# Adaptive max pooling on one core: four halving maxima in place of one reduce instruction

## The chip, the cores and the metric

The kernel runs on one core of a Trainium2 chip. The metric is the time of one execution on the device, in microseconds (us); lower is better. Traces come from the hardware profiler, which records one execution.

## The reference

The input is 32 x 256 x 4096 numbers in float32 (134 MB). Each row of 4096 is cut into 256 groups, and the output holds the maximum of each group (8.4 MB).

```python
def reference(x, output_size):            # x: 32 x 256 x 4096, output_size: 256
    batch, channels, length = x.shape
    result = np.zeros((batch, channels, output_size), dtype=np.float32)
    for i in range(output_size):
        start = int(i * length / output_size)
        end = int((i + 1) * length / output_size)
        result[:, :, i] = np.max(x[:, :, start:end], axis=-1)
    return result
```

4096 divides by 256, so every group has exactly W = 16 neighbouring words. In memory the input is a list of 2,097,152 groups of 16 words, and the output one word for each.

## The kernel before

The groups are dealt to the 128 partitions, 16384 groups to each. They come in 17 loads: a first small one of 128 groups per partition (`FIRST`), then loads of 1024 groups (`CHUNK`; one of them has 1020) and a last one of 900 (`last`). The loads belong to two blocks of the output, `group_a` with the first 14 loads and `group_b` with the last 3. A load of 1024 groups is 64 KB per partition, 8.39 MB in all.

Two tiles lie in SBUF. `ring` takes the loads. It has two halves, each of 1024 + 152 groups (`GAP` = 152), and loads go to the halves in turn. Within a half a load starts at offset 0 or at offset 152, in turn (`moved`). So a load shares all but 152 groups of its place with the load two before it. `kept` takes the maxima of all loads but the last; the maxima of the last load (`last_kept`) are written to the end of its own place in `ring`.

Each full load is pooled in two pieces: first the 872 groups (868 for the load of 1020) that the load two places on will overwrite, then the 152 that it won't. The loop writes this order out (`parts`, or `parts[::-1]` where the load is not moved). The load two places on may be issued when the larger piece is done. The first load and the last are pooled in one piece each. This makes 32 calls of `pooled` (line 56), each one VectorE instruction.

All loads are issued from SyncE's queue (SP; line 96, the first at line 87) and wait there for their place in `ring` to come free. Behind them in the same queue are two stores of `kept` (line 117), one for each block; the second of them waits until the last full load is pooled. The maxima of the last load are stored from ScalarE's queue (ACT; line 114). Line 148 is the end of the program, which waits for all stores. No other engine computes; the tile framework places the waits between dependent instructions.

Of the kernel before, what the change touches and what calls it, by code (L numbers as in the profile page):

```python
# [1 line left out]

# [4 lines left out]


@with_exitstack
def kernel(  # L10
    ctx: ExitStack,
    tc: tile.TileContext,
    x: bass.AP,
    output_size: bass.AP,
    out: bass.AP,
):

    nc = tc.nc
    P = nc.NUM_PARTITIONS
    fp32 = mybir.dt.float32

    B, C, L = x.shape
    O = int(output_size)  # L30
    assert L % O == 0, (L, O)
    W = L // O
    total = B * C * O // P
    assert B * C * O % P == 0

    CHUNK = 1024
    GAP = 152
    FIRST = 128
    LOADS_A, LOADS_B = 13, 2

    LESS = 4
    group_a = [FIRST] + [CHUNK] * (LOADS_A - 1) + [CHUNK - LESS]
    last = total - sum(group_a) - LOADS_B * CHUNK
    group_b = [CHUNK] * LOADS_B + [last]
    assert 0 < last and last * (W + 1) <= CHUNK * W

    pool = ctx.enter_context(tc.tile_pool(name="pool", bufs=1))
    ring = pool.tile([P, 2 * (CHUNK + GAP) * W], fp32, tag="ring", name="ring")
    kept = pool.tile([P, total - last], fp32, tag="kept", name="kept")

    xw = x.flatten_outer_dims().rearrange("r (o w) -> (r o) w", w=W)
    ow = out.flatten_outer_dims().rearrange("r o -> (r o)")

    def pooled(dst, at, n):

        nc.vector.reduce_max(  # L56
            out=dst,
            in_=ring[:, at * W : (at + n) * W].rearrange("p (n w) -> p n w", w=W),
            axis=mybir.AxisListType.X,
        )  # L60

    taken = 0

    def group(n):

        nonlocal taken
        span = slice(taken * P, (taken + n) * P)
        taken += n
        return (
            xw[span].rearrange("(p n) w -> p (n w)", p=P),  # L70
            ow[span].rearrange("(p n) -> p n", p=P),
        )

    stores = []
    n_loads = 0
    base = 0
    for g, loads in enumerate((group_a, group_b)):
        xg, og = group(sum(loads))
        a = sum(loads) if g == 0 else 0
        for n in loads:  # L80
            if g == 0:
                a -= n
            xn = xg[:, a * W : (a + n) * W]
            dst = kept[:, base + a : base + a + n] if n != last else None
            if n == FIRST:

                nc.sync.dma_start(  # L87
                    out=ring[:, CHUNK * W : (CHUNK + n) * W], in_=xn
                )
                pooled(dst, CHUNK, n)  # L90
            else:

                low = n_loads % 2 * (CHUNK + GAP)
                moved = n_loads // 2 % 2
                at = low + moved * GAP
                nc.sync.dma_start(out=ring[:, at * W : (at + n) * W], in_=xn)
                if n != last:
                    cut = CHUNK - GAP if moved else GAP
                    parts = [(0, cut), (cut, n)]
                    for u, v in parts if moved else parts[::-1]:  # L100
                        pooled(dst[:, u:v], at + u, v - u)
                else:
                    end = (at + CHUNK) * W
                    last_kept = ring[:, end - n : end]
                    pooled(last_kept, at, n)
                n_loads += 1
            if g:
                a += n
        full = a - last if g else sum(loads)
        stores.append((og[:, 0:full], kept[:, base : base + full]))  # L110
        base += full
    assert taken == total

    nc.scalar.dma_start(out=og[:, full : full + last], in_=last_kept)
    tc.no_sync_barrier()
    for dst, src in stores:
        nc.sync.dma_start(out=dst, in_=src)


# [1 line left out]
_INS = ['x', 'output_size']  # L121
_OUTS = [((32, 256, 256), 'float32')]

_NUMBERS = {'output_size': 256}


# [26 lines left out]
```

## Time and profile before

| what | value |
|---|---|
| median of 3 runs | 334.94 us (334.91 to 335.06) |
| span of the profiled execution | 333.1 us |
| own time of the profiled execution | not listed apart from the runs; median less span is 1.84 us |
| VectorE (DVE) busy | 276.5 us, 83% of the span, 32 instructions |
| DMA | 142.61 MB, mean 428 GB/s over the span |
| loads' queue (q1) | 98.8% of the 16 DMA engines' span |
| HBM read, written | 134.22 MB, 8.39 MB |

How to read the lines in this document: a row of the instruction groups gives the line of the kernel, the engine, the operation, the tile written and the tile read with their shapes, the number of such instructions, then their busy time in us, the mean of one in ns, and the idle time of the engine just before them with what ended it. A row of DMA issues gives the size and the median time from issue to landing. A row of the timeline gives start, duration, and the instruction or the merged run of instructions. A row of the stretches gives the stretch and its length, the busy time of VectorE and of GpSimd with their instructions, the clock granted to TensorE, the mean busy share of the 16 DMA engines and their GB/s.

### The profile page before, as it was taken

How to read it: one execution, taken by the hardware profiler on the slowest of the kernel's cores; microseconds unless marked ns; L12 is line 12 of the kernel's file. 1: busy time of each engine (PE TensorE's matmuls, PEld its weight loads, DVE VectorE, ACT ScalarE, POOL GpSimd, SP SyncE). 2: the span in 40 equal slices, each digit the busy share in tenths (PEclk: the TensorE clock that was granted, in tenths of full speed). 3: DMA queues.
4: the chain of work that ended last, by engine and by line, in shares of the span. 5: the costliest groups of instructions: out<-in, count | busy, mean ns of one | idle time of the engine just before them, and what ended most of it. 6: DMA issues, size and time to landing. Idle time of an engine off the chain costs nothing.

```text
span 333.1 us, 113 instructions
## 1 busy us (share of the span) xinstructions
DVE 276.5 (83%) x32; POOL 0.2 (0%) x4
## 2 busy tenths in 40 slices
DVE  2009979797997979799797979979797998979993
POOL 0000000000000000000000000000000000000000
DMA  9898989899898989899898989899898989899996
GB/s 378 378 504 378 504 378 496 386 441 441 378 504 378 504 378 496 386 457 425 378 504 378 504 378 504 378 441 441 385 494 377 504 378 504 378 458 443 421 413 285
DMA packets 2880, 142.61 MB, mean 428 GB/s; under 512 B 320, under 2 KB 320, under 8 KB 448
## 3 DMA queue, kind: packets, MB, share of 16 engines
q1 hardware_dynamic: 2736, 142.15, 98.8%
q10 hardware_dynamic: 144, 0.46, 0.3%
HBM read 134.22 MB, written 8.39 MB: 428 GB/s over the span
## 4 chain that ended last, share of the span: by engine, by line
DMA 57%; DVE 36%; DVEq 5%; issue 0%; SPq 0%
DMA ring<-in_x_dram 57%; DVE kept L56 36%; DVEq L148 5%; SPq L87 0%
## 5 line engine op out<-in xcount | busy, mean ns | idle before, releaser
L56 DVE TENSOR_REDUCE kept<-ring 128x152 f32<-128x2432 f32 (+3 forms) x31 | 261.4, 8472 | 51.5 <-DMA ring<-in_x_dram 51.5
L56 DVE TENSOR_REDUCE ring<-ring 128x900 f32<-128x14400 f32 x1 | 15.1, 15144 | 0.0
L134 POOL MEMSET const-bfloat16-1.0<- 128x1 bf16 x1 | 0.1, 102 | 0.0
L134 POOL MEMSET const-uint8-127<- 128x1 uint8 x1 | 0.1, 102 | 0.0
L134 POOL MEMSET const-float32-0.0<- 128x1 f32 x1 | 0.1, 99 | 0.2 <-issue 0.2
L134 POOL MEMSET const-float32-1.0<- 128x1 f32 x1 | 0.1, 99 | 0.0
## 6 DMA issues: line engine op xcount, KB each, us to landing
ring<-in_x_dram SPq DMA_DIRECT2D x1, 8160.0 KB, 23.9
ring<-in_x_dram SPq DMA_DIRECT2D x1, 7200.0 KB, 21.6
out_dram<-kept SPq DMA_DIRECT2D x1, 6718.0 KB, 37.2
ring<-in_x_dram SPq DMA_DIRECT2D x1, 1024.0 KB, 4.7
out_dram<-kept SPq DMA_DIRECT2D x1, 1024.0 KB, 18.1
out_dram<-ring ACTq DMA_DIRECT2D x1, 450.0 KB, 4.2
ring<-in_x_dram SPq DMA_DIRECT2D x14, 24.0
```

The source lines that it names most:

```text
L56: nc.vector.reduce_max(out=dst, in_=ring[:, at * W : (at + n) * W].rearrange("p (n w) -> p n w", w=W), axis=mybir.AxisListType.X,)
L134: nc = _bacc.Bacc("TRN2", target_bir_lowering=False, num_devices=1)
L148: with _tile.TileContext(nc) as tc:
```

## The change

The function `pooled` is rewritten. Instead of one `reduce_max` over the 16 words of each group it issues four `tensor_tensor` maxima on VectorE. The first takes the maximum of words 0 to 7 and words 8 to 15 of each group and writes it over words 0 to 7, in place in `ring`. The second does the same with words 0 to 3 and 4 to 7, the third with 0 to 1 and 2 to 3. The fourth takes the maximum of word 0 and word 1 of each group and writes it to the destination that the reduce wrote to. The pieces, their order, the loads and the stores are the same.

```diff
+    assert W & (W - 1) == 0
     assert 0 < last and last * (W + 1) <= CHUNK * W
...
     def pooled(dst, at, n):
 
-        nc.vector.reduce_max(
-            out=dst,
-            in_=ring[:, at * W : (at + n) * W].rearrange("p (n w) -> p n w", w=W),
-            axis=mybir.AxisListType.X,
-        )
+        win = ring[:, at * W : (at + n) * W].rearrange("p (n w) -> p n w", w=W)
+        half = W // 2
+        while half:
+            nc.vector.tensor_tensor(
+                out=win[:, :, 0:half] if half > 1 else dst.unsqueeze(2),
+                in0=win[:, :, 0:half],
+                in1=win[:, :, half : 2 * half],
+                op=mybir.AluOpType.max,
+            )
+            half //= 2
```

## The prediction

> **What bounds the kernel now.** I read the instruction groups by shape first, because they price VectorE's work.
>
> ```profile
> L56 DVE TENSOR_REDUCE kept<-ring 128x872 f32<-128x13952 f32 x14 | 205.6, 14686 | 44.0 <-DMA ring<-in_x_dram 44.0
> L56 DVE TENSOR_REDUCE kept<-ring 128x152 f32<-128x2432 f32 x15 | 40.1, 2676 | 0.0
> L56 DVE TENSOR_REDUCE ring<-ring 128x900 f32<-128x14400 f32 x1 | 15.1, 15144 | 0.0
> ```
>
> Between the first two rows 11520 more words cost 12010 ns: 1.0425 ns for each word folded in, and about 0.14 us left over for each instruction (2676 - 2432 x 1.0425 = 141 ns). Most idle time of VectorE ends with a load's landing, so next the stretches of the span with their DMA share:
>
> ```profile
> 5.50:312.70 307.20, 261.16 (x31) 0.00 (x0) 1.00 1.00 433
> ```
>
> From the first landing to the last piece the DMA engines are full, at 433 GB/s. A load of 1024 groups (8.39 MB) lands every 19.35 us (half of the 38.7 us that the chain shows for two), and VectorE works on it for 17.28 us. So DMA is the bound. The chain of waits seems to say otherwise:
>
> ```profile
> by line: DMA ring<-in_x_dram 57.5%; DVE kept L56 36.0%; DVEq L148 4.6%; issue 0.1%; SPq L87 0.1%
> ...
> 39.50 24.00 DMA ring<-in_x_dram
> 63.50 0.02 issue
> 63.53 14.70 DVE kept L56
> ```
>
> It alternates: the large piece (14.70) releases the load two places on, and that lands 24.00 us after its issue. But those 24.00 us are only 19.35 of transfer; 4.65 us are start, completion and standing behind the load still under way. The first load, with nothing in front of it, shows start and completion alone:
>
> ```profile
> ring<-in_x_dram SPq DMA_DIRECT2D x1, 1024.0 KB, 4.7
> ...
> out_dram<-kept SPq DMA_DIRECT2D x1, 6718.0 KB, 37.2
> out_dram<-kept SPq DMA_DIRECT2D x1, 1024.0 KB, 18.1
> out_dram<-ring ACTq DMA_DIRECT2D x1, 450.0 KB, 4.2
> ```
>
> Its 1.05 MB take 2.4 us at 433 GB/s, so 4.7 leaves 2.3 us for start and completion. A large piece may therefore end 4.65 - 2.3 = 2.3 us later before the DMA queue runs dry. The end of the span is read from the timeline and the last stretches:
>
> ```profile
> 295.63 17.28 DVE L56 TENSOR_REDUCE kept<-ring 128x872 f32<-128x13952 f32 x2 [2.07 <-DMA ring<-in_x_dram]
> 312.82 15.14 DVE L56 TENSOR_REDUCE ring<-ring 128x900 f32<-128x14400 f32 x1
> 328.00 0.37 ACTq L114 DMA_DIRECT2D out_dram<-ring  x1
> ```
>
> ```profile
> 330.00:331.00 1.00, 0.00 (x0) 0.00 (x0) 1.00 0.93 375
> 331.00:331.20 0.20, 0.00 (x0) 0.00 (x0) 1.00 0.90 360
> 331.20:331.40 0.20, 0.00 (x0) 0.00 (x0) 1.00 1.00 396
> 331.40:331.60 0.20, 0.00 (x0) 0.00 (x0) 1.00 0.34 126
> 331.60:331.80 0.20, 0.00 (x0) 0.00 (x0) 1.00 0.01 0
> ```
>
> Data moves until about 331.5: the two stores of kept, queued behind the loads, and then the store of the last piece, which lands at 332.2. That last store (0.46 MB, 1.1 us) would land 2.3 + 1.1 = 3.4 us after its issue with the queues empty; it took 4.2, so it stood 0.8 us behind the stores of kept. The final piece can end 0.8 us later at no cost; beyond that it sets the end one for one. Ending earlier gains nothing, since the bytes in front still have to move.
>
> The span is 333.1 us and the median of the runs 334.94. The times list no separate time for the profiled execution, so I add the 1.84 us between the two to every span below.
>
> **The change, part by part.** It touches only how VectorE reduces a piece. DMAs, their order and their queues (SP's loads and stores, ACT's last store) stay; no work is added for another engine. Each reduce of n groups, 16n words, becomes four maxima with 8n, 4n, 2n and n results: 32 instructions become 128.
>
> *The first three steps* (14n results) read adjacent words in runs of 8, 4 and 2. The trace has no two-operand instruction. One bound is one result per cycle, 1.04 ns, the reduce's rate of maxima; the other is one word read per cycle, 2.08 ns. I take 1.04, for the reduce's row is a row of maxima on this engine and this data, and keep 2.08 as a rival.
>
> *The last step* (n results) reads one word in every 16 for each operand, a pattern that no row has. Call its price x ns per result. It is at least 1.04, and at most 16.7 (16 words at 1.0425, if it had to pass over all of them as the reduce does). Three regions matter: up to 2.08 (two cycles, one for each operand's separate fetch), from there to 3.03 (where, worked out below, VectorE becomes the bound), and above. The low end is the nearest row, since the engine and the data are the same, but that row reads adjacent words only. That lone words cost more than one cycle is a guess that no row here bears out or denies; I make it because the step needs two of them per result, and take the middle region at its centre, 2.55.
>
> [...]
>
> *Fixed costs.* Each of the four steps reads what the one before wrote, so each waits for its end. Two independent pieces now overlap by 0.08 us (14.686 + 2.676 against 17.28); that is lost. Handovers in the trace take 0.02 (landing to VectorE) to 0.09 us (before the last chain entry). I take 0.14 + 0.03 = 0.17 for a step, between 0.06 (0.14 less the overlap) and 0.23. Behind each waiting step stand only VectorE's later steps; who waits for them is the SP queue with its next load, and ACT's queue with the last store.
>
> *A load of 1024 groups:* 14 x 1024 x 1.0425 ns = 14.95 us; last step 1.024 x 2.55 = 2.61; eight steps at 0.17, less one overlap between the pieces, 1.3. Sum 18.86, against 17.28 before: 1.58 more, and still under 19.35, so DMA covers it. Without that cover it would be 15 x 1.58 = 24 us. VectorE reaches 19.35 where 16.25 + 1.024x = 19.35: x = 3.03.
>
> *The release of a load:* the large piece takes 14 x 872 x 1.0425 = 12.73, plus 2.22, plus 4 x 0.17 = 0.68: 15.63 in place of 14.69. The 0.94 is inside the 2.3 us found above, so the transfers stay back to back.
>
> *The end:* the last full load still lands at 295.6. It is pooled by 295.63 + 18.86 = 314.5; the last load has landed by then. The store of its part of kept goes out at 314.5 instead of 312.9, and this is hidden: the 6.9 MB store in front of it lands at 291.4 + 37.2 = 328.6. The final piece takes 14 x 900 x 1.0425 = 13.14, plus 0.9 x 2.55 = 2.30, plus 0.68: 16.11. Both together 34.97, against 32.33 before (295.63 to 327.96): 2.64 us later, of which 0.8 are covered. **Sum: 334.94 + 2.64 - 0.8 = 336.8 us.** With x from 2.08 to 3.03 this is 335.9 to 337.7; the bounds of the fixed cost (12 steps by -0.11 to +0.06) widen it to 334.9 to 338.4.
>
> **The rivals.**
>
> *The last step is cheap and DMA hides everything.* In general the end is 30.06 + 1.924x us after 295.63. At x = 1.04 that is 32.06, 0.27 earlier than before, which gains nothing as shown; up to x = 1.6 the slip stays within 0.8. The time is 334.9, and up to x = 1.94 it stays within 0.2%. For it: the 100% DMA share, the 2 us idle per load, and that n results are only a fifteenth of the work. Against: the isolated words. Chance 0.25. [...]
>
> *VectorE becomes the bound.* It decides from x = 3.03 on (or from less with dearer waits). At four cycles, x = 4.17: a load takes 14.95 + 4.27 + 1.3 = 20.52, the final piece 13.14 + 3.75 + 0.68 = 17.57. From the first landing at 24.78, 15 loads and the final piece end at 350.2; with 3.4 for the last store, 0.9 to the end of the span and 1.84, 356.3. At x = 3.5 it is 346. For it: only 0.5 us a load is left in my sum. Against: needs three cycles or more for a result. Chance 0.20.
>
> *Both operands share one read per cycle in all four steps.* 30 words a group: 32.0 + 1.3 = 33.3 a load, 28.8 for the final piece: 24.8 + 15 x 33.3 + 28.8 + 3.4 + 0.9 + 1.84 = 559. The reduce row, one word a cycle, doesn't exclude it. Chance 0.05.
>
> *Faster:* every step overlaps and the last bytes move sooner. The bound is 0.8 us, all of what the last store stood in queue; DMA share leaves little. Chance 0.03.
>
> **How the numbers follow.** The forecast's own case, slower through the tail by 0.3 to 1%, has 0.47. A measurement of this kernel can tell about 0.2%, 0.67 us, from no change. Faster 0.03; same 0.25; slower 0.47 + 0.20 + 0.05 = 0.72. The range starts at 334.7, below the hidden case, and reaches into the rival where VectorE binds, to x of about 3.5, 346: left out are the two-cycle rival, the dearer half of the VectorE-bound one and the gain, 0.18.
>
> **What would show it.** Right: four tensor_tensor rows for each piece size; steps with 8n, 4n, 2n results near 1.04 ns per result plus 0.14 us, and the step to n results well above (872 results: 2.4 us instead of 1.05); VectorE idle before a load's first step near 0.5 us instead of 2.07; DMA share 1.00 as before up to about 312; the last store issued near 330.6, landing about 3.4 us later. Wrong: the last step at the rate of the others; or VectorE without idle time and DMA share below 1.00; or a DMA rate below 433 GB/s with VectorE idle, for which I have no price.

## The result and the profile after

The changed kernel takes 348.18 us (median of 4 runs, 346.77 to 348.69) against 334.97 us: ratio 1.0387, 95% interval 1.0374 to 1.0400. The direction was forecast, the size was not: 336.8 was predicted, with a range up to 346.0. That the direction came true is luck, as the time is lost on a path that the prediction held to be covered. The profiled execution has a span of 346.0 us, 12.9 more than before.

VectorE did not become slower. The instruction groups of the changed kernel, by shape (busy time, mean of one in ns, idle time before):

```profile
L60 DVE TENSOR_TENSOR ring<-ring 128x6976 f32<-128x6976 f32 x14 | 103.9, 7425 | 53.9 <-DMA ring<-in_x_dram 53.9
L60 DVE TENSOR_TENSOR ring<-ring 128x3488 f32<-128x3488 f32 x14 | 53.0, 3783 | 0.0
L60 DVE TENSOR_TENSOR ring<-ring 128x1744 f32<-128x1744 f32 x14 | 27.6, 1970 | 0.0
L60 DVE TENSOR_TENSOR kept<-ring 128x872 f32<-128x872 f32 x14 | 23.0, 1645 | 0.0
L60 DVE TENSOR_TENSOR ring<-ring 128x1216 f32<-128x1216 f32 x15 | 21.3, 1418 | 0.0
...
L60 DVE TENSOR_TENSOR kept<-ring 128x152 f32<-128x152 f32 x15 | 6.3, 418 | 0.0
```

The step with 8 results per group costs (7425 - 1418) / (6976 - 1216) = 1.043 ns per result and 0.15 us per instruction. The last step, which reads every 16th word, costs (1645 - 418) / (872 - 152) = 1.70 ns. VectorE is busy for 277.7 us in all, against 276.5 before.

What changed is when a load may be issued. SP's waits, first of the kernel before, then of the changed one (total, times, longest):

```profile
SPq L96 <- DVE kept L56: 205.6, 14, 14.7
```

```profile
SPq L102 <- DVE kept L60: 242.3, 14, 17.4
```

From the landing of a load to the release of the load two places on, 14.7 us (205.6 / 14) have become 17.0 by the chain below, 15.44 + 1.56. The row's 242.3 / 14 is a little more, 17.3, as long as VectorE's whole work on a load; the chain has the load issued at 61.22, 17.0 us after 44.23. The large piece's own four steps are only 14.82 us. Two passages of the chain of waits (start, duration, what) show where the rest comes from:

```profile
44.23 15.44 DVE ring L60 x6
59.67 1.56 DVE kept L60 x2
61.22 22.03 DMA ring<-in_x_dram
83.25 0.02 issue
83.27 15.44 DVE ring L60 x6
98.71 1.63 DVE kept L60 x2
100.34 24.37 DMA ring<-in_x_dram
```

Six steps that write ring stand ahead of the two that write kept: three of the large piece and three of the small one. The order in which the trace has them start on VectorE is this (partitions x groups x results of a group):

```
L60 TensorTensor ring<-ring 128x872x8
L60 TensorTensor ring<-ring 128x152x8
L60 TensorTensor ring<-ring 128x872x4
L60 TensorTensor ring<-ring 128x152x4
L60 TensorTensor ring<-ring 128x872x2
L60 TensorTensor ring<-ring 128x152x2
L60 TensorTensor kept<-ring 128x872
L60 TensorTensor kept<-ring 128x152
```

So the section on the change, above, is wrong where it says that the order of the pieces is the same. The loop in the source keeps it; the order that the tile framework makes of it does not. Here, where a piece is a chain of dependent steps, the other piece's steps stand between them. The large piece now ends just before the small one.

The consequence, in the stretch from the first landing to where the last piece began before, and up to where it begins now (the last two columns are DMA share and GB/s):

```profile
5.50:312.70 307.20, 250.52 (x117) 0.00 (x0) 1.00 0.98 417
5.50:325.50 320.00, 262.38 (x124) 0.00 (x0) 1.00 0.98 416
```

416 GB/s instead of 433, with a share of 0.98: at times the DMA queue runs dry, so that engines have no packet, and packets take longer as well (both are counted below). The last piece begins at 325.5 instead of 312.8, which is nearly all of the 12.9 us. What follows it is as before:

```profile
325.54 15.38 DVE L60 TENSOR_TENSOR ring<-ring 128x7200 f32<-128x7200 f32 x4 [0.98 <-DMA ring<-in_x_dram]
340.95 0.37 ACTq L120 DMA_DIRECT2D out_dram<-ring  x1
```

### The profile page after: what moved, and what is told of

Read it like the earlier page. It is cut to its first block, busy times and chain, and to the rows that moved or that the text cites. A ratio compares the mean times of both kernels' runs of the same rounds, so it can differ in the third digit from the quotient of the medians.

```text
span 346.0 us, 208 instructions
## 1 busy us (share of the span) xinstructions
DVE 277.7 (80%) x128; POOL 0.2 (0%) x4
## 4 chain that ended last, share of the span: by engine, by line
DMA 59%; DVE 39%; SPq 0%; issue 0%
DMA ring<-in_x_dram 59%; DVE ring L60 36%; DVE kept L60 3%; SPq L102 0%; SPq L93 0%
## 5 line engine op out<-in xcount | busy, mean ns | idle before, releaser
L60 DVE TENSOR_TENSOR ring<-ring 128x1216 f32<-128x1216 f32 (+6 forms) x97 | 249.1, 2632 | 63.2 <-DMA ring<-in_x_dram 63.1
L60 DVE TENSOR_TENSOR kept<-ring 128x152 f32<-128x152 f32 (+3 forms) x31 | 29.8, 1009 | 0.0
## 6 DMA issues: line engine op xcount, KB each, us to landing
out_dram<-kept SPq DMA_DIRECT2D x1, 1024.0 KB, 19.4
```

Of the source, the lines that this page charges most:

```text
L60: nc.vector.tensor_tensor(out=win[:, :, 0:half] if half > 1 else dst.unsqueeze(2), in0=win[:, :, 0:half], in1=win[:, :, half : 2 * half], ...
```

## The experiments

Theory: the loss comes from the late release alone. Rival: the maxima, which read two words at a time and write back into ring while loads are written there, disturb the DMA.

**The maxima with each piece's steps kept together** (e1_order).

```diff
                         pooled(dst[:, u:v], at + u, v - u)
+                        tc.no_sync_barrier()
```

> The four maxima, but each piece's four steps are kept together: all four of the large piece, then all four of the small one (in the changed kernel they alternate, so that the large piece ends with the second last of eight instructions). Theory 1 (the late release of the next load is the whole cause): the large piece ends about 14.9 us after its load has landed instead of 17.0, the loads land every 19.35 us again and DMA share is back at 1.00 with 433 GB/s; VectorE takes about 18.1 us a load, since neighbouring steps no longer overlap; the final piece ends about 1.1 us later than with the reduce, of which 0.8 are covered: 335 to 336 us. Rival (the maxima disturb the DMA, because they read two words and write back in place while loads are written): the release doesn't matter, and the time stays at 345 or more.

Measured: 335.75 us, ratio 1.0025 (1.0016 to 1.0034). SP's waits and the DMA stretch of this kernel:

```profile
SPq L102 <- DVE kept L60: 208.7, 14, 14.9
```

```profile
5.50:312.70 307.20, 268.37 (x122) 0.00 (x0) 1.00 1.00 432
```

All but 0.8 of the 13.2 us are back, though every maximum is still there and VectorE is busier in this stretch than in the kernel before (268.37 us against 261.16). The rival falls as the cause of the loss; what is left of it, at most 0.8 us, comes up again below.

**The kernel before, with reduce, the small piece first** (e2_small_first).

```diff
-                    for u, v in parts if moved else parts[::-1]:
+                    for u, v in parts[::-1] if moved else parts:
```

> The kernel before, with reduce, only the order of the two pieces of a load exchanged: the small one first, so the large one ends about 17.3 us after the landing. Theory 1: slow like the changed kernel or a little slower, 347 to 352 us, with idle times of VectorE before a landing well above 2 us and a DMA share below 1.00. Rival (the two-operand maxima disturb the DMA): no change, 335 us.

Measured: 351.55 us, ratio 1.0504 (1.0477 to 1.0530). SP's waits and the DMA stretch:

```profile
SPq L96 <- DVE kept L56: 241.8, 14, 17.3
```

```profile
5.50:312.70 307.20, 245.61 (x30) 0.00 (x0) 1.00 0.97 411
```

Without a single maximum of two operands the same loss appears, and a little more, as the release is a little later still. The order alone does it.

**How much delay is free?** The prediction had worked out 2.3 us of cover. Five kernels with reduce pool a part of the small piece ahead of the large one; `early` is 76, 120, 10, 32 and 54 groups.

```diff
+                    early = 76
+                    if moved:
+                        parts = [(cut, cut + early), (0, cut), (cut + early, n)]
+                    else:
+                        parts = [(0, early), (cut, n), (early, cut)]
-                    for u, v in parts if moved else parts[::-1]:
+                    for u, v in parts:
```

76 groups: 

> The kernel before, with reduce, but 76 of the 152 groups of the small piece are pooled ahead of the large piece: release at about 16.0 us, 1.3 later than before. Theory 1 with the cover of 2.3 us that the prediction worked out: hidden, 335 us. If the cover is smaller than that (1 us or so): 336 to 342. Rival: 335.

120 groups: 

> As the run before, but 120 of the 152 groups go ahead: release at about 16.8 us, 2.1 later than before. Theory 1 with a cover of 2.3 us and a sharp edge: hidden, 335 us. With an edge that is soft, because 16 DMA engines do not run dry at the same moment: 336 to 343. Rival: 335.

10 groups: 

> The kernel before, with reduce; 10 of the 152 groups of the small piece are pooled ahead of the large one: release at about 14.95 us, as in the ordered maxima. If the 0.8 us that the ordered maxima still lost came from the release: 335.5 to 336.4. If it came from the maxima themselves or their longer end: 335.0.

32 groups: 

> As before it with 32 groups: release at about 15.3 us. If there is no cover worth speaking of and the time grows in proportion (the runs from 16.0 to 17.3 give some 5.7 us for each us of delay): 338 to 339. If there is a cover of about 1 us with a steep step behind it: 335 to 336.

54 groups: 

> As before it with 54 groups: release at about 15.7 us. In proportion: 340 to 342. With a cover of 1 us and a step: 335 to 337.

Measured, with the release read from SP's waits (total by times) and the DMA rate of the stretch 5.50 to 312.70 (the ratios are worked out from all runs of both kernels, so they differ a little from quotients of the medians):

| kernel | release after landing, us | GB/s | median, us | ratio (95% interval) |
|---|---|---|---|---|
| before | 14.7 | 433 | 334.94 | 1 |
| 10 groups | 14.9 | 433 | 335.36 | 1.0013 (1.0004 to 1.0021) |
| 32 groups | 15.3 | 430 | 337.03 | 1.0070 (1.0043 to 1.0097) |
| 54 groups | 15.6 | 428 | 341.80 | 1.0205 (1.0192 to 1.0218) |
| 76 groups | 16.0 | 421 | 344.32 | 1.0271 (1.0244 to 1.0299) |
| 120 groups | 16.7 | 418 | 347.62 | 1.0381 (1.0364 to 1.0399) |
| all 152 (e2) | 17.3 | 411 | 351.55 | 1.0504 (1.0477 to 1.0530) |

Release and rate come from one profiled run, which for 54 groups was the fastest of the six (339.10), so its 428 GB/s is high for a median of 341.80.

There is no cover of 2.3 us and no sharp edge. A delay of 0.2 us costs 0.4, 0.6 us costs 2.1, 1.3 us costs 9.3. The expectation of 335 for 76 groups was missed by 9 us, that for 120 groups by 13, and the milder bounds of the two (342 and 343) were too low as well. 32 groups fell between the two cases expected for them; 54 groups came out in proportion, as one of theirs had it. With 17.0 us the changed kernel's 348.18 stands between the last two rows, where its release puts it.

Why the cover is smaller than worked out is seen in part. A late load doesn't always land late by the delay; some land late by 2 us and others hardly at all. In the changed kernel's timeline, the idle time before VectorE's next load (2.07 in the steady state before) varies:

```profile
83.27 15.44 DVE L60 TENSOR_TENSOR ring<-ring 128x6976 f32<-128x6976 f32 x6 [2.05 <-DMA ring<-in_x_dram]
98.63 2.00 DVE L60 TENSOR_TENSOR kept<-ring 128x872 f32<-128x872 f32 x2
105.16 7.42 DVE L60 TENSOR_TENSOR ring<-ring 128x6976 f32<-128x6976 f32 x1 [4.53 <-DMA ring<-in_x_dram]
```

The load that landed at 105.16 came 21.89 us after the one ahead of it, not 19.35. A load of 1024 groups is 128 packets of 64 KB, 8 for each of the 16 DMA engines if they share them evenly (8 x 2.42 = 19.4 us, the interval of the landings). The packet records give a mean of 2421 ns for such a packet before and 2470 ns after; over the 1792 of them on 16 engines this is 1792 / 16 x 0.049 = 5.5 us of the 12.7 lost before the last piece begins. The packets of the two loads of other sizes are longer too, by 1.9 us counted in the same way. Counted from the same records, an engine has no packet for 5.0 us on average up to there, against 0.0 before. So longer packets (7.4 us) cost more than the dry queue itself (5.0). With 32 groups ahead the engines are without a packet for only 0.2 us, and the packets are 2.0 us longer in all: the loss sets in with longer packets. No packet of 64 KB takes over 2.6 us before; after, 163 do, up to 4.0 us, and 151 of them start within 5 us after the issue of a load. Why they are long there was not tried.

**Give the queue more work while it waits** (e10_split_loads). The changed kernel, steps alternating as they were; the part of a load whose place is free already is issued by itself.

```diff
-                nc.sync.dma_start(out=ring[:, at * W : (at + n) * W], in_=xn)
+                cut = CHUNK - GAP if moved else GAP
+                ends = [(0, n)] if n == last else [(0, cut), (cut, n)]
+                for u, v in ends[::-1] if moved else ends:
+                    nc.sync.dma_start(
+                        out=ring[:, (at + u) * W : (at + v) * W],
+                        in_=xn[:, u * W : v * W],
+                    )
```

> The changed kernel with its alternating steps (release still about 17 us), but every load of 1024 groups is issued as two transfers: the 152 groups whose place is free already, in the queue ahead of the release, and the 872 that need it. So 1.25 MB, 2.9 us at 433 GB/s, stand in the queue while it waits. If the loss comes from the queue running dry: DMA share back to 1.00, 335.5 to 336.5. If the late release costs in another way, or the maxima slow the DMA themselves: 345 or more.

Measured: 338.12 us, ratio 1.0096 (1.0082 to 1.0110). A load that landed at 83.19 releases the next one at 100.19, 17.0 us later, as in the changed kernel. Two lines of the timeline, and the DMA stretch:

```profile
83.19 15.44 DVE L60 TENSOR_TENSOR ring<-ring 128x6976 f32<-128x6976 f32 x6 [2.10 <-DMA ring<-in_x_dram]
100.19 59.95 SPq L105 DMA_DIRECT2D ring<-in_x_dram  x8
```

```profile
5.50:312.70 307.20, 263.02 (x124) 0.00 (x0) 1.00 1.01 432
```

10 of the 13.2 us come back with the release as late as in the changed kernel. So the late release costs only because nothing else stands in the queue; both parts of the loss go away together here: the engines are without a packet for 0.3 us, and the packets of the 872 groups take 2064 ns in the mean and in the median alike. This run doesn't tell the two parts apart. The time missed the expected 336.5 by 1.6: loads land every 19.42 us instead of 19.35 (1.1 us over the 16), one lands 0.8 us late (at 122.84, behind an instruction packet, which the next kernels are about), and the last load, which was not split, lands 18.3 us after the one ahead of it, 1.2 more than its 7.37 MB take at 433 GB/s.

**The last 0.7 us.** Two kernels ask what the ordered maxima still lose (0.8 us). In the first (e8_hybrid) the large pieces go back to reduce.

```diff
         half = W // 2
+        if n in (CHUNK - GAP, CHUNK - GAP - LESS):
+            nc.vector.reduce_max(out=dst, in_=win, axis=mybir.AxisListType.X)
+            half = 0
         while half:
...
                         pooled(dst[:, u:v], at + u, v - u)
+                        tc.no_sync_barrier()
```

> The large piece of each full load by one reduce, every other piece (small ones, first and last load) by four maxima, each piece's steps together: release at 14.7 us as before, maxima in VectorE's remaining time and at the end. If the release alone counts: 335.0 (at the end the small piece is 0.5 us and the last piece 0.2 us longer, inside the 0.8 us of cover there). If maxima as such disturb the loads or the end: 335.4 or more.

Measured: 335.66 us, ratio 1.0021 (1.0012 to 1.0029), with a release of 14.7. So 0.7 us are lost without the 0.2 us of release in e1_order and without maxima in the large pieces. By its expectation this run alone would speak for the maxima. But both e1_order and e8_hybrid have a row on their page that the kernel before has not: `q14 instruction: 1, 0.01, 0.0%`. The second kernel (e9_many_reduces) has no maxima of two operands, only more instructions.

```diff
+                        step = v - u if v - u > GAP else 30
+                        for s in range(u, v, step):
+                            e = min(s + step, v)
+                            pooled(dst[:, s:e], at + s, e - s)
-                        pooled(dst[:, u:v], at + u, v - u)
```

> The kernel before, with reduce and the same release (14.7 us); only the small piece of 152 groups is cut into reduces of 30 groups and one of 2, so VectorE has 107 instructions instead of 32. The two kernels with maxima whose release is early both had one 8 KB packet of queue q14 (instructions) in the middle of their span, and a load that landed 0.5 to 0.75 us late behind it. If that packet costs the 0.7 us which they lost: 335.5 to 335.8 here too, without any maximum, and one late landing in the profile. If the maxima or their longer end cost it: 335.0.

Measured: 335.55 us, ratio 1.0021 (1.0012 to 1.0031). The DMA queues in the stretch from 144.5 to 146 us, and the timeline behind it:

```profile
q14 instruction: 1, 0.01, 1.3%
```

```profile
140.79 17.58 DVE L56 TENSOR_REDUCE kept<-ring 128x872 f32<-128x13952 f32 x7 [1.77 <-DMA ring<-in_x_dram]
160.88 17.58 DVE L56 TENSOR_REDUCE kept<-ring 128x872 f32<-128x13952 f32 x7 [2.52 <-DMA ring<-in_x_dram]
180.23 17.58 DVE L56 TENSOR_REDUCE kept<-ring 128x872 f32<-128x13952 f32 x7 [1.77 <-DMA ring<-in_x_dram]
```

The load in flight when the packet passes lands 0.74 us late (20.09 us after the one ahead of it, not 19.35; 2.52 of idle time instead of 1.77), all others are on time, and the 0.7 us are not made up by the end. The same stands in the other traces: the packet passes at 125.78 in e1_order, 183.73 in e8_hybrid and 119.30 in e10_split_loads, and in each the next landing, and no other of a full load, is late, by 0.75, 0.51 and 0.81 us. So the 0.7 us go with the instruction packet that these kernels, which have more instructions, show in mid-span; the profile counts it on the same 16 DMA engines (1.3% of them in the 1.5 us above). The packet itself takes 0.31 us of one engine; why the load is late by more is not shown. The changed kernel has the packet too (at 129.69); how much of its 13.2 us belongs to it is not shown.

## Why the prediction was wrong, point by point

**The bound** was right in that DMA sets the time, only not at the forecast 433 GB/s but at 416, and VectorE's work per load, 17.4 us, stays under 19.35 (17.36 in the timeline from a load's first step to its last).

**The price of the steps.** 1.04 ns per result for the first three and about 0.15 us per instruction (0.17 with the handover was forecast) were right. The last step at x = 2.55 was mis-sized: it is 1.70. That is the side of the rival in which DMA hides everything (up to 1.94). No run shows 2.55: it was a guess, the centre of the region from 2.08 to 3.03. Its direction came true, as the last step, with both operands 16 words apart, costs more per result than the first three (1.70 ns against 1.04); its size did not (872 results take 1645 ns, where 2.55 per result and 0.17 us would give 2394). What the prediction calls a cycle is the 1.0425 ns per word of the reduce's rows; no trace here shows VectorE's clock.

**The overlap between instructions**, which the prediction took as lost between dependent steps, was not lost. The eight steps of a load last 17.91 us by their rows and 17.36 by the timeline: alternating pieces overlap by 0.08 us at each of seven joints. The same alternation moved the release.

**The release of a load** is the step that failed, twice. It put the large piece's end at 15.63 us; with its steps together it would have been 14.9 (208.7 / 14 in e1), and it was 17.0, because the small piece's steps stand between. The prediction took the order of instructions from the source's loop and did not ask what the framework would put between dependent steps. And it set 2.3 us of cover against this, from the 4.7 us of a load that had the queue to itself. The runs show well under 0.6 us. With the measured costs even its own 15.63 would have cost about 7 us (54 groups: 341.80). With the right release and its own cover it would still have found nothing to pay (17.0 - 14.7 = 2.3). So the cover was the larger error, and the order is what made it count: with the steps together the time is 335.75.

**The end** was right in kind, though the changed kernel doesn't show it: there the last piece waits 0.98 us for its load, and the last store is issued at 340.95, not near 330.6. In e1 VectorE takes 33.3 us from the landing of the last full load to the end of the last piece, 1.0 more than before, and the last store lands 3.2 us after its issue instead of 4.2: so there was some cover, near the 0.8 worked out (the store in e8 needs 3.4, the figure predicted for an empty queue).

**The rivals.** The time came close to that of "VectorE becomes the bound", 346 at x = 3.5 (the prediction's own terms sum to 345.4 there), but the mechanism was another: VectorE waited for landings for 63.1 us, more than the 51.5 before. A reader who looked only at the number would have confirmed the wrong rival. No rival had the alternation or the instruction packet. Of the signs that the prediction named, the one that came is a DMA rate below 433 GB/s with VectorE idle, for which it had no price.

## What to carry to other kernels

When one instruction becomes a chain of dependent ones, look at the order in which the chains are issued and at which end of a chain releases a transfer: the work can stay the same and the release still move (from 14.7 to 17.3 us with the same reduces in e2_small_first). Cover that is worked out as time between issue and landing has to be measured with a few delays; here the queue lost rate long before it was empty by that sum (a delay of 0.6 us, of the 2.3 worked out, cost 2.1 us). More instructions were not free here either, with DMA as the bound: one 8 KB instruction packet in mid-span went with 0.6 us (e9_many_reduces).

## What the runs showed of the hardware

- The cost of a late issue set in softly: 0.4 us in the total for 0.2 us of delay per load, 2.1 for 0.6, 9.3 for 1.3, with runs of one kernel spread by up to 3.7 us (32 groups: 335.84 to 339.58) where the kernel before repeats within 0.5 (334.78 to 335.28).
- In the changed kernel, whose queue gets its next load late, rate was lost in two ways: engines without a packet (5.0 us), and 64 KB packets of 2470 instead of 2421 ns in the mean.
- In the changed kernel a two-operand maximum over words 16 apart took 1.70 ns per result, over adjacent pairs and longer runs 1.04.
- The kernels with 83, 107 and 128 VectorE instructions have one 8 KB instruction packet in mid-span, those with 32 and 47 have none. With it and the release as early as before, the total is 0.6 to 0.7 us longer (e9_many_reduces, e8_hybrid).
